# Tree attention on one core: K and Q of heads 16 to 79 laid side by side by GpSimd before TensorE transposes them

## The chip, the cores and the metric

The kernel runs on one core of a Trainium2 chip. A core has five engines that run side by side, each through its own list of instructions in order: TensorE (PE: matmuls and transpositions; its weight loads are shown as PEld), VectorE (DVE), ScalarE (ACT), GpSimd (POOL) and SyncE (SP). Sixteen DMA engines move data between the main memory and the on-chip memory. TensorE writes into PSUM, from where VectorE and ScalarE take its results; everything else lies in SBUF, a memory of 128 partitions.

The metric is the device time of one execution in microseconds (us). The span is the time from the first to the last instruction in the profile; the time of an execution is a little longer.

## The reference

For 8 x 12 = 96 heads, each with 512 positions of 64 numbers, the reference computes softmax attention. A position sees only itself and its ancestors in a binary tree.

```python
for i in range(seq):
    mask[i, i] = 1
    parent = i
    while parent > 0:
        parent = (parent - 1) // 2
        mask[i, parent] = 1

scores = np.einsum('bhqd,bhkd->bhqk', Q, K) * scale
scores = scores + (1 - mask) * (-1e9)

weights = np.exp(scores - np.max(scores, axis=-1, keepdims=True))
weights = weights / (np.sum(weights, axis=-1, keepdims=True) + 1e-10)

return np.einsum('bhqk,bhkd->bhqd', weights, V).astype(np.float32)
```

Inputs and output are float32: 12.6 MB each for Q, K, V and the output.

## The kernel before

**Pairs and steps.** The 96 heads are worked on in 48 pairs, one pair per step `i`. A step has parts that are named by letters: `S` is both score products of pair `i` (`scores1`, `scores2`) with the exponentials on ScalarE, `V` is the value products of pair `i - 1` (`values`, L662) with the normalisation on VectorE (`norm`, L692 and L694), `K` and `Q` are turns. Steps 0 to 8 have lists of their own (`FIRST`); later an odd step is `S V K`, an even one `S V Q`, and step 15 is `S Q V K`. Step 6 is `S K D V Q`: scores of pair 6, a K turn, copies by VectorE, values of pair 5, a Q turn.

**Turns.** The scores need K and Q with the 64 numbers of a position along the partitions. They are loaded with the positions along the partitions, so TensorE transposes them (`turn`, which calls `narrow_k`, `narrow_q`, `wide_k`, `wide_q`, `far_q`), and VectorE copies the result out of PSUM. From pair 8 on a turn serves two pairs. Each transposition loads a piece of K or Q as weights and runs it against a unit matrix. A piece of one head of the pair is 64 columns wide and fills 64 of 128 output partitions; a turn of two pairs takes 16 of these *half* transpositions (L477 for K, L507 and L538 for Q). The K turn in an odd step `i` prepares pairs `i + 3` and `i + 4`, the Q turn in an even step pairs `i + 4` and `i + 5`.

**Blocks and layouts.** K and Q are loaded in blocks of 8 heads: block `b` holds heads `8b` to `8b + 7`, which are pairs `4b` to `4b + 3`. The two heads of a pair do not lie side by side in a loaded block. For blocks 10 and 11 alone `lay_beside` (L445, on GpSimd) copies a block so that they do; the copy takes a buffer of the same pool as the loads. Then one *whole* transposition of 128 columns serves both heads, and a turn takes 8 of them (L470, L532). Heads 0 to 15 are laid out one way, heads 16 to 31 ("wide") a second way, heads 32 to 95 ("far") a third.

**V.** V is loaded in blocks of 16 heads. Before the value products use it, its rows are spread into two working tiles in turn (`vt`, copied at L371 by VectorE, ScalarE and GpSimd). A working tile is written anew for a block only when the values of the block before last are done.

**What sets the order.** The order on each engine is the order in which the program is written; no planner moves anything. GpSimd's own list is written out in `pool_program`: the loads of K, Q and V (which convert float32 to bfloat16 on the way), its share of the spreading, the copies of `lay_beside`, and the stores of finished outputs, in groups of 8 heads. `ready` says from which step on an entry may be emitted; this places it against the other engines' instructions, and GpSimd runs its list strictly in order. `BEHIND` holds the stores back so that loads come first. `NOUT // 2` is the number of output buffers, each of 8 heads. GpSimd's DMAs take eight semaphores in turn, so a DMA waits until the one eight before it has landed. Some of the last stores go out through SyncE's and ScalarE's queues (`store_apart` and the end of the kernel).

The entries of GpSimd's list around the change, before:

```python
(load_q, 28, 4), (load_rows, 2, "leaves0", "leaves1"), (load_k, 32, 8), (load_q, 32, 8),
(load_rows, 3, "upper"),
(spread_pool, (1, "Z0", 8, 16), (1, "Z1", 8, 16), (1, 6, 8, 16), (1, 9, 8, 16)),
(load_q, 40, 8), (load_k, 40, 8), (load_rows, 3, "leaves0", "leaves1"), (load_q, 48, 8),
```

Of the kernel before, what the change touches and what calls it, by code (L numbers as in the profile page):

```python
# [12 lines left out]
NOUT = 22  # L13
# [106 lines left out]
def kernel(  # L120
# [7 lines left out]
    nc = tc.nc  # L128
# [35 lines left out]
    loads = ctx.enter_context(tc.tile_pool(name="loads", bufs=4))  # L164
    vloads = ctx.enter_context(tc.tile_pool(name="vloads", bufs=3))
# [274 lines left out]
    def lay_beside(name, b):  # L440

        kept = ksts if name == "kst" else qsts
        assert all((name, h) in issued for h in range(KB * b, KB * b + KB))
        sides[name, b] = side = loads.tile([P, KB, 4, D], bf16, name=name)
        return nc.gpsimd.tensor_copy(  # L445
            out=side.rearrange("p (s a) t d -> p s a (t d)", a=2).rearrange(
                "p s a (t d) -> p (s a t) d", t=4
            ).rearrange("p (s a) d -> p s a d", a=2).bitcast(int32),
            in_=kept[b].rearrange("p (a x) t d -> p (x t) a d", a=2).bitcast(int32),
        )  # L450

    def both(name, i, slot):

        side = sides[name, i // 4].rearrange("p h t d -> p (h t d)")
        return side[:, 2 * D * slot:2 * D * slot + 2 * D]

    def slots(st, i):
        return st[2 * i // KB].rearrange("p (g x) t d -> p g (x t) d", x=2)

    def wide_k(i):  # L460
        kp = ktp.rearrange("p u c -> p (u c)")
        st = slots(ksts, i)
        place = [2 * i % KB // 2 + a if i < FAR else i % 4 // 2 + 2 * a for a in range(2)]
        for u in range(2):
            for t in range(4):
                mixed = 64 * MIXED[t] + 32 * u
                leaves = 512 + 64 * LEAVES[t] + 32 * u
                dims = (256, 2), (leaves - mixed, 2), (1, 32)
                if ("kst", i // 4) in sides:
                    nc.tensor.transpose(  # L470
                        out=columns(kp, mixed, *dims),
                        in_=both("kst", i, 8 * (i % 4 // 2) + 4 * u + t),
                        identity=ptile[:, 0:128],
                    )
                    continue
                for a in range(2):
                    nc.tensor.transpose(  # L477
                        out=columns(kp[64 * a:64 * a + 64, :], mixed, *dims),
                        in_=st[:, place[a], 4 * u + t, :],
                        identity=ptile[:, 0:128],  # L480
                    )
# [17 lines left out]
    def wide_q(i):  # L499
        qp = qtp.rearrange("p u c -> p (u c)")  # L500
        halves = qp.rearrange("p (b c) -> p b c", b=2)
        st = slots(qsts, i)
        for u in range(2):
            for x, t in enumerate(ORDER):
                c = 256 * u + 64 * x
                for a in range(2):
                    nc.tensor.transpose(  # L507
                        out=halves[64 * a:64 * a + 64, :, c:c + 64],
                        in_=st[:, 2 * i % KB // 2 + a, 4 * u + t, :],
                        identity=ptile[:, 0:128],  # L510
                    )
# [9 lines left out]
    def far_q(i):  # L521
# [5 lines left out]
        st = qsts[j].rearrange("p (g x) t d -> p g (x t) d", x=4)  # L527
        for u in range(2):
            for x, t in enumerate(ORDER):
                c = 128 * u + 32 * x  # L530
                if ("qst", j) in sides:
                    nc.tensor.transpose(  # L532
                        out=quarters[:, :, c:c + 32], in_=both("qst", i, 4 * (2 * last + u) + t),
                        identity=ptile[:, 0:128],
                    )
                    continue
                for a in range(2):
                    nc.tensor.transpose(  # L538
                        out=quarters[64 * a:64 * a + 64, :, c:c + 32],
                        in_=st[:, a, 4 * (2 * last + u) + t, :],  # L540
                        identity=ptile[:, 0:128],
                    )
# [8 lines left out]
    def turn(name, i):  # L551
# [4 lines left out]
        level = (i >= WIDE) + (i >= FAR)  # L556
        {"kst": (narrow_k, wide_k, wide_k), "qst": (narrow_q, wide_q, far_q)}[name][level](i)
# [162 lines left out]
    def pool_program():  # L720
# [17 lines left out]
        for h in range(56, NH, KB):  # L738
# [3 lines left out]
            ops += [(load_q, h, KB)] + top + [(load_k, h, KB)]  # L742
# [25 lines left out]
    def ready(op, i):  # L768
# [158 lines left out]
```

## Time and profile before

| | |
|---|---|
| time, median of 3 runs | 134.0 us (133.42 to 134.24) |
| the profiled execution: its time, its span | 133.38 us, 131.6 us |
| mean granted TensorE clock in it | 0.969 |
| busy: TensorE, VectorE, ScalarE, GpSimd | 114.4, 103.8, 101.1, 83.0 us |
| read from and written to main memory | 37.94 MB, 12.58 MB: 384 GB/s over the span |

The profile page tells how long each engine was busy, the span in 40 slices (each digit is the busy share of a slice in tenths), the chain of work that ended last, and the costliest groups of instructions. A row of the timeline has the start in us, the duration in us, the engine, the line and the operation; behind it, in brackets, how long the engine had been idle just before and what ended that. A row of the windows has, for a stretch of time, the busy time of each engine, the granted clock, the share of the DMA engines and the GB/s that they moved; asked for one engine it has only that one. A row of a group has busy time and mean ns of one instruction, and the idle time just before them.

### The profile page before, as it was taken

To read this page: it belongs to the slowest core of one execution; us is meant where nothing else is said; L and a number is where in the kernel's file an instruction comes from. 1 tells how busy PE (TensorE), PEld (TensorE's weight loads), DVE (VectorE), ACT (ScalarE), POOL (GpSimd) and SP (SyncE) were. 2 spreads that over 40 slices of the span, in tenths; PEclk is the share of its full clock that TensorE was granted. 3 is DMA by queue.
4 is the path that set the end of the run, shared out by engine and by line. 5 is a ranking of instruction groups with operands and counts; after the bars stand their busy time and mean duration, and the time that the engine had idled before them with its cause. 6 is when DMAs were issued, how large, how long until landed. Compare 5 with 4: busy or idle time off the path is not lost.

```text
span 131.6 us, 5435 instructions
## 1 busy us (share of the span) xinstructions
PE 114.4 (87%) x2353; PEld 79.7 (61%) x2353; DVE 103.8 (79%) x254; ACT 101.1 (77%) x163; POOL 83.0 (63%) x114
## 2 busy tenths in 40 slices
PE   6788959999999798899998898997998999999900
PEld 2354745676667566577676575675675777775600
DVE  3459859588999998989899879898899977875440
ACT  4279577689799996959996878896898888789900
POOL 6999524454485999994498799944999935002000
PEclk9999996799999999999999999999999999999975
DMA  2999999999999999999999999999999999999991
GB/s 87 244 195 194 200 196 200 201 202 206 203 201 209 207 207 204 210 206 202 209 206 200 306 269 207 293 282 242 330 221 327 246 288 400 403 398 396 395 345 66
DMA packets 28157, 32.25 MB, mean 245 GB/s; under 512 B 1214, under 2 KB 23358, under 8 KB 28134
## 3 DMA queue, kind: packets, MB, share of 16 engines
q0 software_dynamic: 25696, 29.63, 110.7%
q1 hardware_dynamic: 1878, 1.83, 4.0%
q10 hardware_dynamic: 560, 0.46, 1.3%
q8 instruction: 18, 0.29, 0.8%
q14 instruction: 5, 0.04, 0.1%
HBM read 37.94 MB, written 12.58 MB: 384 GB/s over the span
## 4 chain that ended last, share of the span: by engine, by line
DMA 30%; PE 29%; POOL 17%; DVE 13%; issue 4%; ACT 2%; POOLq 0%; ACTq 0%
DMA kst<-in_K_dram 22%; PE ob L662 9%; POOL vt L371 9%; DMA vst<-in_V_dram 8%; PE s L567 4%; DVE of L694 4%; DVE vt L371 3%; PE s L574 3%; POOL kst L244 2%; POOL qst L244 2%; PE s L612 2%; PE s L601 2%; POOL vst L244 2%; PE qtp L532 2%; PE ktp L470 2%
## 5 line engine op out<-in xcount | busy, mean ns | idle before, releaser
L584 ACT ACTIVATE e<-s 128x1024 bf16<-128x1024 f32 x40 | 40.9, 1022 | 13.2 <-PE s L574 12.7
L662 PE MATMUL ob<-vt,e 128*128 128x65 bf16 (+1 forms) x940 | 37.4, 198 | 1.6 <-DVE of L694 1.1
L662 PEld LDWEIGHTS <-e 128*128 128x128 bf16 (+1 forms) x960 | 30.4, 103 | 9.5 <-PE s L612 1.1
L371 POOL COPY vt<-vst 32x512 int32<-32x512 int32 (+4 forms) x44 | 32.5, 740 | 5.2 <-PE ob L662 3.0
L618 ACT ACTIVATE e<-s 128x384 bf16<-128x384 f32 x80 | 34.7, 490 | 0.0
L694 DVE TENSOR_TENSOR of<-ob,rec 128x512 f32<-128x512 f32 x47 | 32.5, 692 | 1.6
L371 DVE COPY vt<-vst 32x1024 bf16<-32x1024 bf16 (+5 forms) x47 | 21.4, 456 | 2.6 <-DMA vst<-in_V_dram 1.8
L692 DVE RECIPROCAL rec<-ob 128x8 f32<-128x8 f32 x47 | 9.6, 205 | 10.7 <-PE ob L662 9.8
L702 POOL DMA_DIRECT2D out_dram<-of x11 | 9.9, 898 | 9.1 <-DVE of L694 8.7
L574 PE MATMUL s<-qq,kq 64*128 64x512 bf16 x80 | 15.3, 377 | 0.0
L612 PE MATMUL s<-qq,kq 64*128 64x160 bf16 (+1 forms) x320 | 14.8, 208 | 0.4 <-issue 0.4
L612 PEld LDWEIGHTS <-kq 64*128 64x128 bf16 x320 | 12.3, 94 | 4.7 <-issue 0.6
L567 PE MATMUL s<-far,codes 40*128 40x512 bf16 x64 | 12.5, 386 | 0.1
L580 ACT ACTIVATE e<-s 128x1024 bf16<-128x1024 f32 x8 | 8.2, 1022 | 5.6 <-PE s L574 5.5
L254 POOL DMA_DIRECT2D qst<-in_Q_dram x12 | 8.4, 704 | 6.3 <-DMA kst<-in_K_dram 3.4
L601 PEld LDWEIGHTS <-codes 40*128 40x128 bf16 x80 | 6.4, 94 | 9.5 <-issue 3.9
L543 DVE COPY qq<-qtp 128x1024 bf16<-128x1024 bf16 x16 | 10.9, 682 | 0.7 <-PE qtp L538 0.7
L254 POOL DMA_DIRECT2D kst<-in_K_dram x11 | 8.4, 764 | 4.3 <-DMA vst<-in_V_dram 1.7
L477 PE MATMUL ktp<-ptile,kst 128*64 128x128 bf16 x256 | 9.9, 220 | 1.2 <-DMA kst<-in_K_dram 0.6
L601 PE MATMUL s<-far,codes 40*128 40x384 bf16 x64 | 10.6, 324 | 0.4 <-ACT e L618 0.3
L371 ACT COPY vt<-vst 32x512 int32<-32x512 int32 (+3 forms) x19 | 10.4, 546 | 0.6 <-DMA vst<-in_V_dram 0.2
L299 POOL DMA_DIRECT2D vst<-in_V_dram x7 | 5.6, 800 | 6.4 <-DMA vst<-in_V_dram 4.5
(56 smaller groups left out, 157.2 us busy)
## 6 DMA issues: line engine op xcount, KB each, us to landing
out_dram<-of POOLq DMA_DIRECT2D x10, 1024.0 KB, 16.4
kst<-in_K_dram POOLq DMA_DIRECT2D x9, 512.0 KB, 14.3
qst<-in_Q_dram POOLq DMA_DIRECT2D x8, 512.0 KB, 16.3
vst<-in_V_dram POOLq DMA_DIRECT2D x12, 256.0 KB, 14.0
vst<-in_V_dram POOLq DMA_DIRECT2D x6, 512.0 KB, 13.0
qst<-in_Q_dram POOLq DMA_DIRECT2D x6, 256.0 KB, 12.1
kst<-in_K_dram POOLq DMA_DIRECT2D x4, 256.0 KB, 10.8
out_dram<-of SPq DMA_DIRECT2D x3, 256.0 KB, 6.0
```

What stands on the lines that cost most here:

```text
L254: return nc.gpsimd.dma_start(out=kept[b][:, h0 % KB:h0 % KB + n, :, :].rearrange("p (g x) t d -> p g (x t d)", x=x), in_=src[:, h0 // x:(h ...
L371: return copy(out=dst, in_=src)
L477: nc.tensor.transpose(out=columns(kp[64 * a:64 * a + 64, :], mixed, *dims), in_=st[:, place[a], 4 * u + t, :], identity=ptile[:, 0:128],)
L543: nc.vector.tensor_copy(out=qqs[j][:, :, 8 * last:8 * last + 8, :].rearrange("p b u c -> p b (u c)"), in_=quarters,)
L567: nc.tensor.matmul(out=sp[:, a, :], lhsT=(k1code if i < WIDE else k1wide)[64 * a:64 * a + CODE_ROWS, :], rhs=(q1code, q1wide, q1far)[(i >= ...
L574: nc.tensor.matmul(out=sp[:, a, :], lhsT=keys(i, a, TOP), rhs=qTs[i][64 * a:64 * a + 64, :, :].rearrange("p t c -> p (t c)"), start=False, ...
L584: ) if i < WIDE else nc.scalar.activation(
L601: nc.tensor.matmul(out=flat[:, a, :, :].rearrange("p u (t c) -> p u t c", t=4)[:, :, :, 32 // n:], lhsT=k2wide[64 * a:64 * a + CODE_ROWS, ...
L612: nc.tensor.matmul(out=flat[:, a, :, lo:hi], lhsT=keys(i, a, WTILE2[t]), rhs=qT[64 * a:64 * a + 64, :, lo:hi], start=False, stop=t == 1, s ...
L618: nc.scalar.activation(out=e2s[i % NE][:, a, :, 32:128].rearrange("p t (r u) -> p t r u", u=n), in_=flat[:, a, :, :].rearrange("p u (t r) ...
L662: nc.tensor.matmul(out=ob[lo:hi, a, 65 * t:65 * t + 65], lhsT=e[:, a, PLACE[t], lo:hi], rhs=vt[vtile[tile_v][0]][:, head(i, a) % VB, vtile ...
L694: nc.vector.tensor_tensor(out=ofs[j][:, h0:h1 + 1:head(i, 1) - head(i, 0), :, :], in0=o4[:, a:a + n, :, 0:D], in1=rec[:, a:a + n, :, :].to ...
```

## The change

GpSimd lays K and Q of blocks 2 to 9 side by side too, as it did with blocks 10 and 11. The copies get a pool of their own (`beside`, two buffers for K and two for Q). The blocks of heads 16 to 31 are laid in two halves, because there the two heads of a pair lie closer together. With this `wide_k`, `wide_q` and `far_q` lose their path of half transpositions: every turn from pair 8 on takes 8 whole ones. TensorE has 4204 instructions for 4720. GpSimd's list gets the new entries: blocks 2 to 5 at written places, then for each block `b` from 8 on the laying of Q and K of block `b - 2`, just behind the load of Q of block `b` and ahead of the spreading of V and the load of K. The load of Q of heads 56 to 63 moves ahead of rows of V of heads 64 to 79. The output buffers go from 11 to 9.

```diff
-NOUT = 22
+NOUT = 18
...
+    beside = ctx.enter_context(tc.tile_pool(name="beside", bufs=2))
...
-        sides[name, b] = side = loads.tile([P, KB, 4, D], bf16, name=name)
-        return nc.gpsimd.tensor_copy(
-            out=side.rearrange("p (s a) t d -> p s a (t d)", a=2).rearrange(
-                "p s a (t d) -> p (s a t) d", t=4
-            ).rearrange("p (s a) d -> p s a d", a=2).bitcast(int32),
-            in_=kept[b].rearrange("p (a x) t d -> p (x t) a d", a=2).bitcast(int32),
-        )
+        sides[name, b] = side = beside.tile([P, 16, 2, D], bf16, name=f"{name}side")
+        if KB * b >= 2 * FAR:
+            return nc.gpsimd.tensor_copy(
+                out=side.bitcast(int32),
+                in_=kept[b].rearrange("p (a x) t d -> p (x t) a d", a=2).bitcast(int32),
+            )
+        for m in range(2):
+            nc.gpsimd.tensor_copy(
+                out=side[:, 8 * m:8 * m + 8, :, :].bitcast(int32),
+                in_=kept[b][:, 4 * m:4 * m + 4, :, :].rearrange(
+                    "p (a x) t d -> p (x t) a d", a=2
+                ).bitcast(int32),
+            )
...
     def wide_k(i):
...
-                for a in range(2):
-                    nc.tensor.transpose(
-                        out=columns(kp[64 * a:64 * a + 64, :], mixed, *dims),
-                        in_=st[:, place[a], 4 * u + t, :],
-                        identity=ptile[:, 0:128],
-                    )
+                nc.tensor.transpose(
+                    out=columns(kp, mixed, (256, 2), (leaves - mixed, 2), (1, 32)),
+                    in_=both("kst", i, 8 * (i % 4 // 2) + 4 * u + t),
+                    identity=ptile[:, 0:128],
+                )
...
     def wide_q(i):
...
-                for a in range(2):
-                    nc.tensor.transpose(
-                        out=halves[64 * a:64 * a + 64, :, c:c + 64],
-                        in_=st[:, 2 * i % KB // 2 + a, 4 * u + t, :],
-                        identity=ptile[:, 0:128],
-                    )
+                nc.tensor.transpose(
+                    out=halves[:, :, c:c + 64], in_=both("qst", i, 8 * (i % 4 // 2) + 4 * u + t),
+                    identity=ptile[:, 0:128],
+                )
...
-            (load_rows, 3, "upper"),
+            (lay_beside, "kst", 2), (lay_beside, "qst", 2), (load_rows, 3, "upper"),
             (spread_pool, (1, "Z0", 8, 16), (1, "Z1", 8, 16), (1, 6, 8, 16), (1, 9, 8, 16)),
-            (load_q, 40, 8), (load_k, 40, 8), (load_rows, 3, "leaves0", "leaves1"), (load_q, 48, 8),
+            (load_q, 40, 8), (load_k, 40, 8), (lay_beside, "kst", 3), (lay_beside, "qst", 3),
+            (load_rows, 3, "leaves0", "leaves1"), (load_q, 48, 8),
             (spread_top, 2), (spread_pool, (2, "Z0", 0, 16), (2, "Z1", 0, 16)), (load_k, 48, 8),
-            (spread_pool, (2, "X", 0, 16), (2, "M", 0, 16), (2, "D1", 0, 16)), (spread_top, 3, 0, 12),
+            (lay_beside, "kst", 4), (lay_beside, "qst", 4),
+            (spread_pool, (2, "X", 0, 16), (2, "M", 0, 16), (2, "D1", 0, 16)),
+            (load_q, 56, 8), (lay_beside, "qst", 5), (lay_beside, "kst", 5), (spread_top, 3, 0, 12),
             (load_rows, 4, "upper"), (spread_top, 3, 12, 16),
...
-            ops += [(load_q, h, KB)] + top + [(load_k, h, KB)]
+            beside = [(lay_beside, name, h // KB - 2) for name in ("qst", "kst")]
+            ops += ([(load_q, h, KB)] + beside if h > 56 else []) + top + [(load_k, h, KB)]
...
         if f is lay_beside:
-            return 2 * (i + 3) >= KB * (args[1] + 2) + KB - 4 * KB
+            return args[1] < 4 or i >= 4 * args[1] - 8
...
         if f is load_rows:
-            return 2 * i >= VB * (args[0] - 2)
+            return i >= {4: 12, 5: 17}.get(args[0], 8 * (args[0] - 2))
```

More of the change, by code (lines that the diff above doesn't have):

```diff
@@ L443, in lay_beside @@
         assert all((name, h) in issued for h in range(KB * b, KB * b + KB))
-        sides[name, b] = side = loads.tile([P, KB, 4, D], bf16, name=name)
-        return nc.gpsimd.tensor_copy(
-            out=side.rearrange("p (s a) t d -> p s a (t d)", a=2).rearrange(
-                "p s a (t d) -> p (s a t) d", t=4
-            ).rearrange("p (s a) d -> p s a d", a=2).bitcast(int32),
-            in_=kept[b].rearrange("p (a x) t d -> p (x t) a d", a=2).bitcast(int32),
-        )
+        sides[name, b] = side = beside.tile([P, 16, 2, D], bf16, name=f"{name}side")
[11 more added lines that the diff above has]
+            )
     def both(name, i, slot):
[L454 to L458, printed above, removed]
+        return sides[name, i // 4][:, slot, :, :].rearrange("p a d -> p (a d)")
     def wide_k(i):
         kp = ktp.rearrange("p u c -> p (u c)")
-        st = slots(ksts, i)
-        place = [2 * i % KB // 2 + a if i < FAR else i % 4 // 2 + 2 * a for a in range(2)]
         for u in range(2):
@@ L467, in wide_k @@
                 leaves = 512 + 64 * LEAVES[t] + 32 * u
[L468 to L472, printed above, removed]
-                        identity=ptile[:, 0:128],
-                    )
-                    continue
-                for a in range(2):
-                    nc.tensor.transpose(
-                        out=columns(kp[64 * a:64 * a + 64, :], mixed, *dims),
-                        in_=st[:, place[a], 4 * u + t, :],
-                        identity=ptile[:, 0:128],
-                    )
+                nc.tensor.transpose(
[3 more added lines that the diff above has]
+                )
         kk = work.tile([P, 2, 20, 32], bf16, name="kq")
@@ L501, in wide_q @@
         halves = qp.rearrange("p (b c) -> p b c", b=2)
-        st = slots(qsts, i)
         for u in range(2):
@@ L530, in far_q @@
                 c = 128 * u + 32 * x
[L531 to L542, printed above, removed]
+                nc.tensor.transpose(
+                    out=quarters[:, :, c:c + 32], in_=both("qst", i, 4 * (2 * last + u) + t),
+                    identity=ptile[:, 0:128],
+                )
         nc.vector.tensor_copy(
@@ L556, in turn @@
         level = (i >= WIDE) + (i >= FAR)
+        assert not level or (name, i // 4) in sides, (name, i)
         {"kst": (narrow_k, wide_k, wide_k), "qst": (narrow_q, wide_q, far_q)}[name][level](i)
```

4 lines of the change are left out of this document (removed).

## The prediction

> **What bounds the kernel now.** I read the page first (its parts 1 and 2), then the chain of waits, then the timeline of TensorE and GpSimd around the places that the chain names.
>
> ```profile
> PE 114.4 (87%) x2353; PEld 79.7 (61%) x2353; DVE 103.8 (79%) x254; ACT 101.1 (77%) x163; POOL 83.0 (63%) x114
> POOL 6999524454485999994498799944999935002000
> DMA  2999999999999999999999999999999999999991
> ```
>
> The DMA row is full from the second slice to the last but one: the transfers never run dry. TensorE has the most busy time, and GpSimd (POOL), the engine that the change loads, is the least busy. But its row is uneven: slices 14 to 18, 21 to 26 and 29 to 32 are nearly full.
>
> ```profile
> 65.02 18.93 DMA kst<-in_K_dram
> 84.00 0.64 PE ktp L477 x16
> ...
> 90.39 0.61 POOL vt L371
> ...
> 99.85 1.05 POOL qst L445
> 100.94 0.62 PE qtp L532 x8
> ```
>
> In the chain a K load is issued at 65.02 and lands 18.9 us later; TensorE then turns it at 84.00. From 90.39 to 100.9 the chain runs on GpSimd: it spreads V for heads 80 to 95, then lays Q block 10 beside itself (L445), and TensorE starts on that block right behind it.
>
> ```profile
> 81.42 0.68 PE L538 MATMUL qtp<-ptile,qst 128*64 128x128 bf16 x16 [0.61 <-DMA qst<-in_Q_dram]
> 93.84 0.64 PE L477 MATMUL ktp<-ptile,kst 128*64 128x128 bf16 x16 [0.29 <-DMA kst<-in_K_dram]
> 100.94 0.62 PE L532 MATMUL qtp<-ptile,qst 128*128 128x128 bf16 x8 [0.60 <-POOL qst L445]
> 120.00:125.00 5.00, 4.88 (x102) 3.30 (x98) 2.47 (x6) 4.58 (x9) 0.59 (x1) 1.00 1.01 392
> 128.00:132.00 4.00, 0.00 (x0) 0.00 (x0) 0.00 (x0) 0.00 (x0) 0.00 (x0) 0.50 0.22 75
> ```
>
> So three things are nearly level here. TensorE meets Q block 8 at 81.42 and K block 9 at 93.84 just as they land; it meets Q block 10 at 100.94 just as GpSimd has laid it; and from there it is busy without a hole (4.88 of 5.00 us in the window from 120) while the DMA share stays at 1.01. No gain in one of them alone can shorten the span by much; a delay of GpSimd's laying reaches TensorE at once.
>
> **The change part by part.**
>
> *Transpositions.* 32 turns (16 of K, 16 of Q, for blocks 2 to 9) go from 16 half transpositions to 8 whole ones: 256 pairs of weight load and matmul fewer. Blocks 10 and 11 are laid already, so both kinds stand in this trace:
>
> ```profile
> 85.47 0.79 PE L662 MATMUL ob<-vt,e 128*128 128x65 bf16 x20
> 86.10 0.61 PE L538 MATMUL qtp<-ptile,qst 128*64 128x128 bf16 x16
> 86.64 0.39 PE L567 MATMUL s<-far,codes 40*128 40x512 bf16 x2
> ...
> 102.40 0.79 PE L662 MATMUL ob<-vt,e 128*128 128x65 bf16 x20
> 103.12 0.62 PE L470 MATMUL ktp<-ptile,kst 128*128 128x128 bf16 x8
> 103.67 0.39 PE L567 MATMUL s<-far,codes 40*128 40x512 bf16 x2
> ...
> 105.29 0.62 PE L532 MATMUL qtp<-ptile,qst 128*128 128x128 bf16 x8
> ```
>
> From start to start, 16 halves take 86.64 - 86.10 = 0.54 us, 8 wholes 103.67 - 103.12 = 0.55. And the value products ahead of them hold TensorE 0.63 us with halves behind, 0.72 with wholes. A turn thus gets no cheaper, but 0.1 us dearer: 32 turns, at most 3 us, all of it inside the waits below, so I put nothing in the sum for it.
>
> The Trainium skill's page "TensorE: Matmul & The Clock Gate", section "Back-to-back issue gap", gives about 81 ns per load-and-matmul pair at 128 columns in a stream; by it 8 pairs fewer would save an estimated 0.65 us a turn. The trace has 34 ns for a half and 69 for a whole, so here the count of instructions is not what a turn costs. The Trainium skill's page "TensorEngine Tiling (Array Packing)", section "Key Properties", says that two column tiles load and multiply in parallel and that a change of tiling drains the array, and the value products end on 64-column tiles; both speak against this change, and the 0.54 beside 0.55 and the 0.63 beside 0.72 agree.
>
> *Copies.* GpSimd gets 20 more: 8 of half a block (blocks 2 and 3), 12 of a whole one (blocks 4 to 9).
>
> ```profile
> L445 POOL COPY kst<-kst 128x1024 int32<-128x1024 int32 x2 | 2.1, 1046 | 1.7 <-DMA kst<-in_K_dram 1.7
> L371 POOL COPY vt<-vst 32x512 int32<-32x512 int32 x18 | 11.2, 621 | 3.9 <-PE ob L662 3.0
> 32.63:84.74 52.11, 41.65 (x59) 1.00 1.25 219
> ```
>
> A whole one is 1.05 us by its own row. A half one has no row; bounds are half of that, 0.52, and 0.62, the row of another copy of the same length; I take 0.62. Together 12 x 1.05 + 8 x 0.62 = 17.5 us on GpSimd, in order with its loads and its spreading.
>
> *The first wait.* The copies of block 2 stand behind the issue of the Q load of heads 32 to 39. In the built program each GpSimd DMA waits for the one eight before it to land.
>
> ```profile
> 26.98 0.64 PE L477 MATMUL ktp<-ptile,kst 128*64 128x128 bf16 x16
> ...
> 19.84 0.70 POOL L254 DMA_DIRECT2D qst<-in_Q_dram  x1 [0.65 <-DMA kst<-in_K_dram]
> DMA to landing us min/median/max: 11.5/11.5/11.5
> ...
> 31.93 0.70 POOL L254 DMA_DIRECT2D qst<-in_Q_dram  x1 [0.51 <-PE s L612]
> ```
>
> For that load the one eight before was issued at 19.84 and took 11.5 us: it landed at 31.3, the load went out from 31.93 to 32.63, and earlier it cannot go. The first half of K block 2 is then laid at 33.3. TensorE turned that K at 26.98 (pairs 8 and 9, step 6) straight from the load. Now it waits for 33.3: 6.3 us. Behind this turn in TensorE's order stand the values of pair 5, the Q turn and all scores; VectorE's copies, ScalarE's exponentials and the stores wait for those.
>
> *The second wait, which covers the first.* From 32.63 on GpSimd has no pause left. Its work of before up to the issue of Q block 10's load (84.04 to 84.74) is 41.65 us in that window; the after kernel puts 8 halves (5.0) and 9 wholes (Q and K of 4 to 7, Q of 8; 9.4) among it before Q block 8 is laid. With the pause of 0.04 to 0.06 us that the timeline has between two copies (some 45 times, 2 us): 32.6 + 41.65 + 5.0 + 9.4 + 2 = 90.7, so TensorE turns Q block 8 at about 91.0 where it did at 81.42: 9.6 us later. TensorE itself, 6.3 us late, would have been there at about 87 (80.8 without its own wait, plus 6.3), so it waits some 4 us more. The idle time of 10.5 us in that window (52.11 - 41.65) was all the room that GpSimd had, and the added 16.4 us don't fit in.
>
> *The third wait.* Four steps later the chain of before is met again.
>
> ```profile
> 90.39 4.86 POOL L371 COPY vt<-vst 32x512 int32<-32x512 int32 x6 [3.04 <-PE ob L662]
> ```
>
> GpSimd may spread V for heads 80 to 95 only when the values of pair 31 are done; then follow 6 copies, the load of K block 11, 3 copies, a store and the laying of Q block 10, and TensorE goes on at 100.94: 10.55 us. After: Q block 8 at 91.0, four steps of 2.18 us (from 103.12 to the next such turn at 105.29 it is 2.17) give 99.7; the values are done 0.2 earlier, 99.5; plus 10.6 is 110.1. TensorE alone would be there at 108.4, so it waits 1.7 us; before, the same place cost 0.60. Later blocks have room: Q block 11 is needed four steps on.
>
> *The tail.* From this turn to the end of the span it was 131.6 - 100.94 = 30.7 us, TensorE without a hole. It is the same work after, so the span is 110.1 + 30.7 = 140.8. The profiled execution has 1.8 us around its span (133.38 for 131.6): **142.6 us**, +9.2 on the profiled execution, which lies 0.6 us under the median of 134.0. I say 142.5.
>
> *At nothing.*
>
> ```profile
> 59.84 0.91 POOL L702 DMA_DIRECT2D out_dram<-of  x1
> out_dram<-of POOLq DMA_DIRECT2D x10, 1024.0 KB, 16.4
> 79.48 0.77 POOL L254 DMA_DIRECT2D kst<-in_K_dram  x1
> DMA to landing us min/median/max: 14.3/14.3/14.3
> ...
> 95.21 0.77 POOL L254 DMA_DIRECT2D kst<-in_K_dram  x1
> DMA to landing us min/median/max: 13.9/13.9/13.9
> ...
> 111.82 0.62 PE L470 MATMUL ktp<-ptile,kst 128*128 128x128 bf16 x8
> ```
>
> Two output buffers fewer: the tenth block of outputs (pairs 36 to 39, from about 101) now waits for the first store, issued at 59.84 with some 16.4 us to land: 25 us of room; only a store that much later would cost, and the same sum as above puts it 8 later. K and Q buffers free earlier: loads are held by the eight-before rule, not by buffers. Q block 7's load is moved ahead of V rows of heads 64 to 79: the same bytes through a full queue. K block 9's load goes out at 85.6 by the sum, 6.1 late, of 14.3 us to land, most of which is queue: it is hidden. K block 11's goes out at 105.4, 10.2 late of 13.9; here the queue runs dry for some us, and K block 11 lands perhaps 3 us late, at 112; it is needed at 111.8 + 9.2 = 121. If this cover were gone, the 3 us would show.
>
> **The rivals.**
>
> 1. *Only the last chain stays* (GpSimd's copies go quicker than I add, or fit into its pauses). K block 9 still lands no earlier than 93.8, by the wait of TensorE for it at 93.84; its laying, 1.05 us, stands ahead of the spreading of heads 80 to 95: 94.9 + 10.6 = 105.5 for 100.94, +4.5: **137.9**. For it: TensorE and VectorE could win back what step 6 lost. Against: the sum of rows has no such room.
>
> 2. *GpSimd hinders VectorE.*
>
> ```profile
> L371 DVE COPY vt<-vst x12: 416/532/909, 62.4 to 97.7; 32x1024 bf16<-32x1024 bf16 x12
> L371 DVE COPY vt<-vst 32x1024 bf16<-32x1024 bf16 x28 | 14.7, 527 | 1.0 <-DMA vst<-in_V_dram 0.4
> ```
>
> The same copy took 416 to 909 ns while GpSimd was busy about it. If all 28 such copies took 0.909 for their mean of 0.527, VectorE had 10.7 us more; between none and all of it would show, I take half, 5: **147.5**. The Trainium skill's page "Advanced Engine Details and Errata", section "VectorE Performance Modes", says that the second port is shared and that both block each other. The spread of that row agrees; what it costs is not seen.
>
> 3. *Faster: the instruction count rules.* If a whole transposition cost the 34 ns of a half one, a turn would fall by 0.27 us, 32 turns by 8.7 us.
>
> ```profile
> 125.00:128.00 3.00, 0.34 (x10) 0.17 (x5) 1.35 (x5) 0.00 (x0) 0.00 (x0) 0.81 0.97 355
> ```
>
> TensorE would then regain the lost steps, and the end would be the queue's: it is still full here (0.97), and 0.22 x 4.00 = 0.9 us of transfers are left behind 128. Packed they end at 128.9, so between 0 and 2.7 us are to be had; I take half, 1.4: **132.0**. It decides from the point at which GpSimd lays a block before TensorE asks for it, which at 26.98 against 33.3 it doesn't, and the two transposition rows speak against the price.
>
> 4. *The change does nothing measurable*, because waits and gains cancel under the full queue: **134**. The build has 4204 TensorE instructions for 4720, so it is made; only the 6.3 us at step 6 would have to vanish.
>
> **How the numbers follow.** Forecast 0.68 (140 to 146), rival 1 0.14, rival 2 0.11, rival 3 0.03, rival 4 0.04. The range goes from 137.5 (rival 1, with 0.4 for its copies) to 147.5 (rival 2), which leaves out 3 and 4 and the edges. About 1% is what a measurement of this kernel can tell from no change. Slower by over 1%: 0.93; within: 0.04; faster: 0.03.
>
> **What will show it.** Right, if TensorE's first whole K turn waits some 6 us for GpSimd, if Q block 8 is turned near 91 behind GpSimd, if GpSimd's row is full from slice 10 to 32 with about 100 us busy, and if 8 wholes again take 0.55. The DMA row should have its first holes after slice 30. Wrong, if GpSimd's copies of 128 partitions take far from 1.05, if it shows pauses between 33 and 90, or if TensorE regains its steps between 35 and 80.

## The result, and the profile after

The changed kernel takes 146.07 us (median of 6 runs, 144.66 to 146.61) where the kernel before takes 133.78 us (6 runs on the same chip): a ratio of 1.0905, 95% interval 1.0869 to 1.0942. It is slower by 12.3 us. Forecast were 142.5 us, from 137.5 to 147.5. The profiled execution took 146.32 us with a span of 144.5. In some kernels below the executions scatter by 1 to 3%; the ratios leave out those that lie over 1.5% above the fastest of their kernel, while medians and ranges take in all, so that the two need not agree.

First the page of the changed kernel: busy times, three rows of the span in 40 slices (3.6 us each), and the chain that ended last.

```profile
PE 119.1 (82%) x2097; PEld 83.8 (58%) x2097; DVE 109.0 (75%) x254; ACT 101.1 (70%) x163; POOL 100.2 (69%) x134
POOL 7989353556999999929999999995199995200200
PEclk9999999965999999699999999969999999999997
DMA  4999999999999999998999999999993999993473
POOL 30%; PE 24%; DMA 22%; DVE 16%; issue 4%; ACT 2%; POOLq 0%; ACTq 0%
```

GpSimd is busy 17.2 us more (100.2 for 83.0), and its row is full from slice 11 to 33, but for two breaks (18, and 28 and 29). It is the first engine of the chain, with 30%. The DMA row, full to the end before, now has a hole in slice 31 (108.4 to 112.0 us) and thins out from slice 37 on: the loads run out while GpSimd is late to issue the next (K block 11, in the timeline at 108.92). TensorE has 256 pairs of instructions fewer and is still busy 4.7 us longer (119.1 for 114.4). The PEclk row tells most of the reason: it drops to 5 or 6 in three places ahead of the end (slices 9 and 10, 17, 27); before, it drops to 6 and 7 in one (slices 7 and 8). The whole transpositions have a part in it too: in the experiment below that has them without any copy TensorE is busy 115.4 us at a granted clock of 0.983, in the kernel before with fewer output buffers 112.7 at 0.984.

Next the waits of the changed kernel (us in all, times, the longest).

```profile
PE ktp L469 <- POOL kstside L452: 7.5, 1, 7.5
POOL vt L372 <- PE ob L643: 7.3, 2, 4.8
PE qtp L519 <- POOL qstside L447: 4.0, 2, 2.6
```

TensorE waits three times for a laid block, 7.5 us once and 4.0 in two. GpSimd in turn waits twice for TensorE, 7.3 us. In the timeline (start, duration, engine, line; in brackets the idle time before and what ended it) these are the places:

```profile
31.85 0.70 POOL L255 DMA_DIRECT2D qst<-in_Q_dram  x1 [0.43 <-issue]
32.55 1.17 POOL L452 COPY kstside<-kst 128x512 int32<-128x512 int32 x2
33.23 1.03 PE L469 MATMUL ktp<-ptile,kstside 128*128 128x128 bf16 x8 [7.55 <-POOL kstside L452]
36.22 0.85 POOL L300 DMA_DIRECT2D vst<-in_V_dram  x1 [1.40 <-issue]
64.25 1.38 POOL L372 COPY vt<-vst 32x128 int32<-32x128 int32 x4 [2.58 <-PE ob L643]
93.02 1.03 POOL L447 COPY qstside<-qst 128x1024 int32<-128x1024 int32 x1
94.11 0.62 PE L519 MATMUL qtp<-ptile,qstside 128*128 128x128 bf16 x8 [2.57 <-POOL qstside L447]
104.15 4.81 POOL L372 COPY vt<-vst 32x512 int32<-32x512 int32 x6 [4.76 <-PE ob L643]
108.92 0.77 POOL L255 DMA_DIRECT2D kst<-in_K_dram  x1
113.59 1.07 POOL L447 COPY qstside<-qst 128x1024 int32<-128x1024 int32 x1
114.72 0.62 PE L519 MATMUL qtp<-ptile,qstside 128*128 128x128 bf16 x8 [1.48 <-POOL qstside L447]
```

TensorE stands from 25.68 until the first half of K block 2 is laid, then before Q block 8 and before Q block 10. Between the first two, GpSimd stops only at 36.22 and at 64.25. The second stop is for the values of pair 15, which TensorE delivers 11.3 us later than before (step 16 in the table below).

The granted clock, by windows (the last columns are PEclk, DMA share and GB/s):

```profile
29.81:36.64 6.83, 3.41 (x40) 2.79 (x42) 2.29 (x7) 0.00 (x0) 4.16 (x7) 0.50 1.32 203
57.12:60.53 3.41, 3.41 (x44) 2.37 (x42) 3.16 (x7) 2.41 (x4) 3.14 (x6) 0.50 1.18 205
94.66:98.07 3.41, 3.41 (x43) 2.35 (x41) 2.60 (x4) 2.25 (x4) 3.41 (x5) 0.50 1.07 338
```

Behind waits TensorE runs at half speed: 10.2 us of its busy time lie in these windows (3.41 in each), where the granted clock is 0.50. By the clock alone, the same work at the full one would take about half of that, an estimate. From the score matmul of step 29 (94.66) to that of step 30 (98.28) it takes 3.62 us, to the next (100.46) the usual 2.18:

```profile
94.66 0.61 PE L548 MATMUL s<-far,codes 40*128 40x512 bf16 x2
98.28 0.39 PE L548 MATMUL s<-far,codes 40*128 40x512 bf16 x2
100.46 0.39 PE L548 MATMUL s<-far,codes 40*128 40x512 bf16 x2
```

The start of the first score matmul of some steps, before and after, shows where the time was lost (the column on the right is an experiment below):

| step | before | after | lost | after, TensorE kept busy in two waits |
|---|---|---|---|---|
| 7 | 28.71 | 36.18 | 7.5 | 35.54 |
| 16 | 51.54 | 62.81 | 11.3 | 62.18 |
| 28 | 79.08 | 89.84 | 10.8 | 89.19 |
| 29 | 82.03 | 94.66 | 12.6 | 94.00 |
| 30 | 84.57 | 98.28 | 13.7 | 96.18 |
| 37 | 101.49 | 115.27 | 13.8 | 113.92 |
| 47 | 122.28 | 136.77 | 14.5 | 134.98 |
| span | 131.6 | 144.5 | 12.9 | 141.9 |

### The profile page after: what moved, and what is told of

Its sections match the earlier page's. It is cut to its first block, busy times and chain, and to the rows that moved or that the text cites. A ratio compares the mean times of both kernels' runs of the same rounds, so it can differ in the third digit from the quotient of the medians.

```text
span 144.5 us, 4942 instructions
## 1 busy us (share of the span) xinstructions
PE 119.1 (82%) x2097; PEld 83.8 (58%) x2097; DVE 109.0 (75%) x254; ACT 101.1 (70%) x163; POOL 100.2 (69%) x134
## 4 chain that ended last, share of the span: by engine, by line
POOL 30%; PE 24%; DMA 22%; DVE 16%; issue 4%; ACT 2%; POOLq 0%; ACTq 0%
DMA vst<-in_V_dram 17%; POOL vt L372 14%; PE ob L643 8%; DVE vt L372 6%; DMA kst<-in_K_dram 5%; DVE of L675 4%; PE qtp L519 3%; PE s L548 3%; POOL qstside L447 3%; PE ktp L469 2%; PE s L555 2%; PE s L593 2%; POOL kst L255 2%; POOL qst L255 2%; PE s L582 2%
## 5 line engine op out<-in xcount | busy, mean ns | idle before, releaser
L643 PE MATMUL ob<-vt,e 128*128 128x65 bf16 (+1 forms) x940 | 38.5, 200 | 4.1 <-DVE of L675 2.5
L643 PEld LDWEIGHTS <-e 128*128 128x128 bf16 (+1 forms) x960 | 31.5, 104 | 12.2 <-DVE of L675 3.3
L372 DVE COPY vt<-vst 32x1024 bf16<-32x1024 bf16 (+5 forms) x47 | 26.9, 571 | 3.0 <-DMA vst<-in_V_dram 2.1
L469 PE MATMUL ktp<-ptile,kstside 128*128 128x128 bf16 x160 | 13.1, 228 | 7.9 <-POOL kstside L452 7.5
L683 POOL DMA_DIRECT2D out_dram<-of x11 | 9.8, 891 | 12.3 <-DVE of L675 12.3
L673 DVE RECIPROCAL rec<-ob 128x8 f32<-128x8 f32 x47 | 9.6, 204 | 11.3 <-PE ob L643 10.9
L593 PEld LDWEIGHTS <-kq 64*128 64x128 bf16 x320 | 12.3, 96 | 4.8 <-issue 0.6
L469 PEld LDWEIGHTS <-kstside 128*128 128x128 bf16 x160 | 9.7, 102 | 8.8 <-POOL kstside L452 7.7
L478 DVE COPY kq<-ktp 128x256 bf16<-128x256 bf16 x20 | 8.3, 415 | 8.3 <-PE ktp L469 8.3
L519 PE MATMUL qtp<-ptile,qstside 128*128 128x128 bf16 x128 | 10.3, 226 | 4.0 <-POOL qstside L447 4.0
L372 ACT COPY vt<-vst 32x512 int32<-32x512 int32 (+3 forms) x19 | 10.4, 545 | 1.2 <-DMA vst<-in_V_dram 0.8
## 6 DMA issues: line engine op xcount, KB each, us to landing
vst<-in_V_dram POOLq DMA_DIRECT2D x12, 256.0 KB, 10.8
vst<-in_V_dram POOLq DMA_DIRECT2D x6, 512.0 KB, 11.3
kst<-in_K_dram POOLq DMA_DIRECT2D x4, 256.0 KB, 10.2
```

Of the source, the lines that this page charges most:

```text
L372: return copy(out=dst, in_=src)
L469: nc.tensor.transpose(out=columns(kp, mixed, (256, 2), (leaves - mixed, 2), (1, 32)), in_=both("kst", i, 8 * (i % 4 // 2) + 4 * u + t), id ...
L519: nc.tensor.transpose(out=quarters[:, :, c:c + 32], in_=both("qst", i, 4 * (2 * last + u) + t), identity=ptile[:, 0:128],)
L593: nc.tensor.matmul(out=flat[:, a, :, lo:hi], lhsT=keys(i, a, WTILE2[t]), rhs=qT[64 * a:64 * a + 64, :, lo:hi], start=False, stop=t == 1, s ...
L643: nc.tensor.matmul(out=ob[lo:hi, a, 65 * t:65 * t + 65], lhsT=e[:, a, PLACE[t], lo:hi], rhs=vt[vtile[tile_v][0]][:, head(i, a) % VB, vtile ...
```

## The experiments

The theory: the time is lost in waits for blocks that GpSimd lays late, in a list that it runs in order; the clock goes down behind waits. The rivals: GpSimd's copying hinders VectorE by itself; the new transpositions cost or gain; the output buffers. Ratios are to the kernel before, timed beside it.

**The transpositions alone.** `lay_beside` is left out, and the whole transpositions read the loads as they lie.

```diff
-        return sides[name, i // 4][:, slot, :, :].rearrange("p a d -> p (a d)")
+        kept = ksts if name == "kst" else qsts
+        flat = kept[i // 4].rearrange("p h t d -> p (h t d)")
+        return flat[:, 2 * D * slot:2 * D * slot + 2 * D]
```

> The changed kernel without any laying: the 8 whole transpositions of a turn read the loaded block as it lies, so K and Q go to the scores in a wrong order; no copy is made, none is waited for. It measures the form of the transpositions alone. Theory: 8 wholes cost TensorE as much as 16 halves and 0.1 us more a turn: 133.5 to 136, no gain. Rival (the count of instructions is what a turn costs): 132.5 or less, and a step of 1.9 us instead of 2.1.

132.84 us, ratio 0.9946 (0.9904 to 0.9988), just under the 133.5 to 136 that I had expected. The timeline of this kernel, in a stretch without waits:

```profile
112.34 0.39 PE L549 MATMUL s<-far,codes 40*128 40x512 bf16 x2
114.51 0.39 PE L549 MATMUL s<-far,codes 40*128 40x512 bf16 x2
```

A step takes 2.18 us with whole transpositions; with halves the shortest take 2.07. Fewer instructions don't make a step shorter. The half per cent that this kernel gains lies close to what can be told from no change, and it has neither the four copies of before nor the new ones.

**No laying at all, halves everywhere** (the kernel before without the copies of blocks 10 and 11).

```diff
-        return ops
+        return [op for op in ops if op[0] is not lay_beside]
```

> The kernel before without any laying: blocks 10 and 11 too are transposed in halves straight from their loads. Theory (a whole transposition saves nothing and costs 0.1 us a turn, the laying of Q block 10 holds TensorE for 0.6 us): steps 37 to 43 take 2.09 us and not 2.18, TensorE ends some 1.2 us earlier, the full transfer queue gives back part of it: 132.3 to 133.4 for 133.6. Rival (whole transpositions were a gain in the last blocks): 134.5 or more.

133.37 us, ratio 1.0016 (0.9997 to 1.0035). The page:

```profile
PE 112.5 (85%) x2414; PEld 78.9 (60%) x2417; DVE 103.6 (79%) x254; ACT 101.2 (77%) x163; POOL 79.6 (60%) x110
DMA  2999999999999999999999999999999999999992
```

GpSimd is busy 3.4 us less than before, and nothing comes of it. TensorE's 112.5 us for 114.4 are no gain from it: the next kernel, which lays blocks 10 and 11 as before, has 112.7 us, and both profiles lack the half clock of slices 7 and 8 that the one before has. Nor does TensorE end earlier, as I had expected: step 47 starts at 123.60, before at 122.28. The DMA row is full, and the span is that of before, 131.6 us. So there seems to have been little to gain here for a change that eases TensorE.

**Two output buffers fewer alone** (before, `NOUT = 18` for 22).

> The kernel before with 9 output buffers for 11, alone. Theory: the tenth buffer's store has landed 25 us before it is needed; no change, 133 to 134.5. Rival (VectorE waits for stores): 135 or more.

133.29 us, ratio 0.9999 (0.997 to 1.0029): nothing.

**The copies alone.** GpSimd's list of the changed kernel, with all copies; TensorE turns halves straight from the loads, so nothing waits for a copy.

```diff
-                nc.tensor.transpose(
...
+                if False:
+                    nc.tensor.transpose(
...
+                for a in range(2):
+                    nc.tensor.transpose(
```

(The same in all three places that turn K or Q; the first branch is never taken.)

> GpSimd's program is that of the changed kernel, all 24 copies included, but nobody reads what they write: TensorE transposes in halves straight from the loads. It takes the wait for the laid block away and leaves GpSimd's load. Theory (the loss is in the waits for laid blocks): TensorE meets Q block 8 at 84 to 87 and Q block 10 at about 101 to 103; 134.5 to 137.5. Rival (a full GpSimd alone costs, by late loads and late spreading, or by slower copies on VectorE): 140 or more.

137.09 us (135.27 to 139.27), ratio 1.0169 (1.0146 to 1.0192). The profiled execution is the one of 139.27 us. Groups of VectorE by form, first this kernel, then the changed one (busy us, mean ns):

```profile
L373 DVE COPY vt<-vst 32x1024 bf16<-32x1024 bf16 x28 | 18.4, 658 | 0.9 <-DMA vst<-in_V_dram 0.4
```

```profile
L372 DVE COPY vt<-vst 32x1024 bf16<-32x1024 bf16 x28 | 18.1, 646 | 1.9 <-DMA vst<-in_V_dram 1.4
```

Before, these 28 took 527 ns each. So with 20 copies more on GpSimd the copies of VectorE are about a quarter slower, whether or not anybody waits for what GpSimd copies. By the ratio GpSimd's load by itself is worth 1.7%, by the median of all four runs 2.8%; most of the 9.1% needs somebody who waits for the laid blocks.

How the load can cost time is seen in the profiled execution. Three copies of VectorE that took 1.02 us before (first row) take 2.20 while GpSimd lays Q block 2 and spreads V; the value products wait for them:

```profile
33.75 1.02 DVE L371 COPY vt<-vst 32x1024 bf16<-32x1024 bf16 x3
34.42 2.20 DVE L373 COPY vt<-vst 32x1024 bf16<-32x1024 bf16 x3
36.68 0.89 PE L676 MATMUL ob<-vt,e 128*128 128x65 bf16 x20 [1.68 <-DVE vt L373]
```

A stretch of 6.8 us at a granted clock of 0.50 follows, then another wait for VectorE of 1.64 us and a second stretch. Step 16 begins at 57.60 for 51.54, 6.1 us later, with no wait for a laid block. The executions of 135.27 and 135.85 us can't have lost that much in the end, and no profile shows them.

**One wait at a time.** Three kernels lay only some of the blocks, in the places that the changed kernel has for them; the other blocks are turned by halves. First only blocks 2, 3, 10 and 11:

```diff
+LAID = (2, 3, 10, 11)
...
+                if ("kst", i // 4) in sides:
...
-        return ops
+        return [op for op in ops if op[0] is not lay_beside or op[2] in LAID]
```

> The changed kernel with only blocks 2, 3, 10 and 11 laid. The first wait stays (7.5 us, and a slower clock behind it), GpSimd has 12 copies fewer. Theory that the second wait covers the first but that the first alone would also cost: TensorE loses some 8 us at step 6 and wins back at most the 2.5 us that it waited for transfers before: 138 to 140. Rival (the lost time is won back by step 36, and only the full GpSimd counts): 134 to 135.5.

142.14 us, ratio 1.0653 (1.0619 to 1.0687).

```profile
33.53 1.03 PE L475 MATMUL ktp<-ptile,kstside 128*128 128x128 bf16 x8 [7.55 <-POOL kstside L453]
30.08:36.91 6.83, 3.38 (x40) 0.50 1.32 202
```

The first wait and its half clock are there in full, and blocks 2 and 3 alone are worth 6.5%: eight copies of 0.6 us, for the first of which TensorE stands 7.55 us. That is more than the 138 to 140 that I had expected: TensorE is 7.8 us late at step 7, wins nothing back, and is 10.4 us late at step 16.

Then blocks 4 to 11, without the first wait (`LAID = range(4, 12)`), in two experiments:

> The changed kernel, with blocks 2 and 3 transposed in halves straight from their loads again: GpSimd has 8 half copies fewer and TensorE has nothing to wait for at step 6. Theory (GpSimd full, then the chain behind the landing of K block 9): the first wait is gone; Q block 8 is laid 4.9 us earlier than in the sum, at about 86, and Q block 10 at about 105; some 138.5 us (137.5 to 140.5). Rival (the first wait and the slow clock behind it are the whole loss): 134 to 136. Rival (whole transpositions and copies hinder TensorE and VectorE everywhere): 142 or more.

> Blocks 4 to 11 are laid, once more. By the waits: TensorE stands about 5.5 us before K block 4 at about 45 and some 3.4 us before Q block 8 at about 87, each with a stretch of half clock of 6.8 us; 141 to 142.5 us. By a rival, in which the half clock came by itself in that one execution: the waits, and no half clock behind them, 137 to 139.

142.25 us, ratio 1.0628 (1.0569 to 1.0687), not the 138.5 that I had expected; the single execution of the second experiment took 141.63. The time is what I had given to a rival, that whole transpositions and copies hinder everywhere (142 or more), but the transpositions alone cost nothing and the copies alone 1.7%. The timeline and windows of the second (TensorE alone: busy, PEclk, DMA share, GB/s):

```profile
50.97 1.03 PE L475 MATMUL ktp<-ptile,kstside 128*128 128x128 bf16 x8 [5.25 <-POOL kstside L448]
90.58 0.62 PE L545 MATMUL qtp<-ptile,qstside 128*128 128x128 bf16 x8 [3.47 <-POOL qstside L448]
47.62:54.45 6.83, 3.48 (x38) 0.50 1.23 207
92.00:95.41 3.41, 3.41 (x41) 0.50 1.09 326
```

My expectation took away one wait and kept the others as they were. But TensorE, now on time, comes to K block 4 before it is laid and stands there for 5.25 us: a wait that the changed kernel doesn't have, because there the first one has made TensorE late enough. Waits cover each other, so they don't add: 6.5% for blocks 2 and 3, 6.3% for blocks 4 to 11, and 9.1% for both.

Then only blocks 8 to 11 (`LAID = range(8, 12)`), in two experiments:

> The changed kernel with only blocks 8 to 11 laid (before: 10 and 11), blocks 2 to 7 in halves. Theory: GpSimd has time, and only the laying of K block 9 behind its landing, ahead of the spreading of V for heads 80 to 95, is left: Q block 10 some 4.5 us later than before, 138 us (136.5 to 139). Rival (the first wait, or a full GpSimd, is the whole loss): 133.5 to 134.5.

> Only blocks 8 to 11 are laid, once more. By the waits: TensorE stands about 5.4 us before Q block 8 from about 81, since GpSimd lays that block only behind the spreading of V, at 85.3; 138 to 139 us, and the same places as before. By a rival, in which that wait came from a late landing in one execution: no wait there, and a time of 135 to 136.

138.53 us, ratio 1.0373 (1.0334 to 1.0412); 138.98 in the second experiment, whose timeline is:

```profile
81.11 2.77 POOL L373 COPY vt<-vst 32x1024 int32<-32x1024 int32 x3
83.83 0.91 POOL L716 DMA_DIRECT2D out_dram<-of  x1
84.73 0.70 POOL L256 DMA_DIRECT2D qst<-in_Q_dram  x1
85.48 1.03 POOL L448 COPY qstside<-qst 128x1024 int32<-128x1024 int32 x1
86.57 1.03 PE L545 MATMUL qtp<-ptile,qstside 128*128 128x128 bf16 x8 [6.90 <-POOL qstside L448]
97.19 4.80 POOL L373 COPY vt<-vst 32x512 int32<-32x512 int32 x6 [1.91 <-PE ob L676]
```

The time was as expected, but not by the cause that I had in mind (the last chain, behind K block 9). GpSimd is not overloaded here: Q block 8 waits because three spreading copies, a store and a load stand ahead of it in the list. TensorE stands 6.90 us (5.42 in the profile of the first experiment), and the spreading of heads 80 to 95 starts at 97.19 for 90.39.

**The place in the list.** If so, moving the one copy must help. In the kernel with blocks 8 to 11, Q block 8 is laid two spreading copies, a store and a load earlier:

```diff
-                ops.append((spread_pool, *[(o, part, 0, 16) for part in ("X", "M", "D1")]))
+                ops.append((spread_pool, (o, "X", 0, 16)))
+                if h == 72:
+                    ops.append((lay_beside, "qst", 8))
+                ops.append((spread_pool, *[(o, part, 0, 16) for part in ("M", "D1")]))
```

(The copy of Q block 8 at its old place is left out.)

> Blocks 8 to 11 alone are laid, and Q block 8 is laid two spreading copies, a store and a load earlier in GpSimd's list, as soon as it has landed (81.6). By the place in GpSimd's list: TensorE turns Q block 8 at about 83 for 86.4, with at most one stretch of half clock behind it; then the laying of K block 9 at its landing (94.8), which stands ahead of the spreading of heads 80 to 95, sets the next wait: spreading from 95.9, Q block 10 at 105.5 to 106.5, 136 to 137.3 us. By the amount of copying (the same copies, in whatever place, hinder the others): 138 to 138.8, no change against blocks 8 to 11 as they were.

And the same with K block 9 turned by halves, without its copy:

> As with Q block 8 laid earlier, and K block 9 is not laid but turned from its load by halves: 7 copies are left. By the place in GpSimd's list: the spreading of heads 80 to 95 no longer stands behind K block 9; it starts with the values of pair 31, at about 92.5, Q block 10 at 102.5 to 103.5, 134 to 135.3 us. By the amount of copying: one copy of 1.05 us in eight fewer, at most 0.6 us less than blocks 8 to 11, 138.

The first took 139.46 us (137.21 to 140.57, before 134.0), ratio 1.0282 (1.022 to 1.0345). The median of its four times lies above both expectations and is no lower than that of blocks 8 to 11, and the interval touches theirs, so by its time this kernel doesn't settle it. Its profile, of the execution of 140.45 us, has the places as expected: the wait before Q block 8 is down to 2.04 us,

```profile
82.59 1.04 PE L545 MATMUL qtp<-ptile,qstside 128*128 128x128 bf16 x8 [2.04 <-POOL qstside L448]
```

the spreading starts at 96.01 behind K block 9, and Q block 10 is laid from 105.43. But now TensorE waits 3.54 us for that block, and 6.8 us at half clock follow. The second kernel took 136.66 (134.17 to 138.48), ratio 1.0194 (1.0136 to 1.0251), clearly under 1.0373; its median lies between the two expectations. Its profiled execution is the one of 134.17 us:

```profile
80.89 1.11 POOL L448 COPY qstside<-qst 128x1024 int32<-128x1024 int32 x1
82.06 1.03 PE L545 MATMUL qtp<-ptile,qstside 128*128 128x128 bf16 x8 [2.04 <-POOL qstside L448]
92.99 4.80 POOL L373 COPY vt<-vst 32x512 int32<-32x512 int32 x6 [1.12 <-PE ob L676]
102.42 1.07 POOL L448 COPY qstside<-qst 128x1024 int32<-128x1024 int32 x1
```

There the steps are where the place predicts them: the wait before Q block 8 is 2.04 us for 6.90 (or 5.42), the spreading starts at 92.99 (expected 92.5), Q block 10 is laid from 102.42. One copy moved and one left out are together worth 1.8%; the runs don't divide this between the two. Why the other executions of these two kernels are 2 to 4 us longer stays open.

**The half clock alone.** The changed kernel, with matmuls whose results nobody uses put into the first and the second wait (28 ahead of the K turn in step 6, 9 ahead of the Q turn in step 28).

```diff
+            if step == "Q" and i == 28:
+                spin("s1", 9)
...
+            if step == "Y":
+                spin("s1", 28)
```

> The changed kernel, with matmuls of zeros on TensorE in two of its waits: 28 of 512 columns ahead of the K turn of step 6 and 9 ahead of the Q turn of step 28. Their results are not used. It keeps TensorE busy while it waits and so tells what the half clock behind the waits costs. Theory (3 to 4 us of the loss is the half clock; of the first wait's part most is hidden by the full GpSimd): no half clock at 30 to 36 and at 95, step 29 takes 2.2 us and not 3.6; 143 to 145 in place of 146. Rival (the waits alone are the loss): 145.5 to 146.5.

143.94 us, ratio 1.081 (1.0789 to 1.0831), for 1.0905 (1.0869 to 1.0942).

```profile
33.83 0.62 PE L469 MATMUL ktp<-ptile,kstside 128*128 128x128 bf16 x8 [0.48 <-POOL kstside L452]
94.00 0.39 PE L548 MATMUL s<-far,codes 40*128 40x512 bf16 x2
96.18 0.39 PE L548 MATMUL s<-far,codes 40*128 40x512 bf16 x2
55.99:59.40 3.41, 3.41 (x42) 0.50 1.16 208
```

The waits are about as long as they were (the first K turn at 33.83 for 33.23), but the clock stays up behind them: step 29 takes 2.18 us for 3.62. One stretch at half clock is left, at 55.99. By the medians 2.1 us, by the ratios 1.3 us, are thus not waiting but slow running after two of the waits, less than the 3 to 4 that I had put on it.

## Why the prediction was right, and where it was off

The direction was right and the time within the range, 3.6 us above the forecast of 142.5. It lies just above the 140 to 146 of the forecast itself; what the range holds beyond that came from rival 2.

*Transpositions*: right. 8 wholes take 94.66 - 94.11 = 0.55 us from their start to that of the scores behind them, and the whole turns alone make no step shorter. Rival 3, that the count of instructions rules, is out.

*Copies*: right. 20 copies added 17.2 us to GpSimd (17.5 forecast).

*The first wait*: right in place, cause and size: K block 2 is laid and turned at 33.23 (33.3), 6.25 us later than before, behind the load of Q that is issued at 31.85. The half clock behind it, which the sum didn't have, brings the loss to 7.5 us at step 7.

*The second wait, which covers the first*: right in kind, 3.1 us short: Q block 8 is turned at 94.11, not at 91.0. GpSimd's work was as added up, but not "has no pause left":

```profile
32.55:93.02 60.47, 54.64 (x75) 0.94 1.19 214
```

The columns are the busy time of GpSimd, PEclk, DMA share and GB/s. With the laying of Q block 8 (1.03) it is 55.67 us of work, where the sum had 56.05 (41.65 + 5.0 + 9.4); the pauses are 60.47 - 54.64 = 5.83 us, where I took 2. Two of them, 1.40 and 2.58, make 3.98; a pause between 33 and 90 was among the prediction's own signs of being wrong. The larger is GpSimd waiting for the values of pair 15, 11.3 us later than before. The first wait with its half clock accounts for 7.5 of these. By an estimate from these numbers, with 7.5 alone the values would have been done 3.8 us earlier, and GpSimd, which was ready 2.58 us earlier, would not have paused: the pause needs both parts. The other 3.8 us are lost between steps 7 and 16, where the prediction put nothing:

```profile
41.40 2.05 DVE L372 COPY vt<-vst 32x1024 bf16<-32x1024 bf16 x3
52.28 2.01 DVE L372 COPY vt<-vst 32x1024 bf16<-32x1024 bf16 x2
```

Before, these copies of VectorE took 1.02 and 1.04 us (33.75, 42.93). Now GpSimd lays Q block 3 beside the first, and lays Q block 4 and then spreads V beside the second. TensorE waits for VectorE, 0.90 us at 43.51 and 1.71 at 55.30; the stretch at half clock at 57.12 follows. No run takes these 3.8 us apart, but the profiled execution of the kernel with the copies alone, its longest, loses 6.1 us up to step 16 in the same way. I treated the two waits as one covering the other; in fact the first wait, together with the slower copies of VectorE, feeds the second through the spreading of V. The same losses make TensorE itself late: it is ready for Q block 8 at 94.11 - 2.57 = 91.54, where the prediction had it at about 87. Had GpSimd been as early as forecast, TensorE would have been the later of the two, so that a forecast for this place came near is in part luck.

*The third wait*: right as a chain, wrong by what goes before. From the spreading at 104.15 to the turn at 114.72 it is 10.6 us, as forecast. But it starts at 104.15, where the sum had 99.5: 3.1 us from the second wait, and 1.4 from step 29 at half clock, which the sum didn't have at all (0.1 is left over). The step of the prediction that failed here is "four steps of 2.18 us": one of them took 3.62.

*The tail*: 144.5 - 114.72 = 29.8 us, 30.7 forecast; from the start of step 47 to the end of the span it is 7.7 us for 9.3, and no run shows what shortened it. 3.1 + 1.4 + 0.1 - 0.9 = 3.7 us is what the span lies above the forecast of 140.8.

*At nothing*: the output buffers are confirmed by the kernel with `NOUT = 18`. The late loads of K were hidden too: among the waits of the changed kernel TensorE has none for K block 9 or 11.

*Rival 1*, only the last chain, fell: the waits ahead of that chain stay, and its condition, that GpSimd's copies fit into its pauses, isn't met. *Rival 2*, GpSimd hinders VectorE, is there beside the forecast rather than in its place: VectorE's 28 copies took 18.1 us for 14.7, and the kernel with the copies alone loses 1.7%. I had given it 5 us as a case of its own. The Trainium skill's page "Advanced Engine Details and Errata", section "VectorE Performance Modes", says that the two share a port and block each other; the rows agree, with 646 ns for 527. How much of the 12.3 us this is can't be read off: it is part of the 3.8 us above, and the rest lies inside the waits.

## What to carry to other kernels

Before work goes to an engine that is idle on average, write down where in its list the work will stand and when the consumer asks for it: eight copies of 0.6 us, behind a load that went out no earlier than 31.85, cost 6.5% here, while the same engine had 37% of its time free. A copy belongs in the list at the point where its input lands: for Q block 8 that took the wait from 6.90 us to 2.04. Take waits together, not one by one: without the first, the next one appears. Ask whom the copying engine slows down meanwhile, here VectorE. And price a turn from start to start in the trace, not by its count of instructions.

## What the runs showed of the hardware

Short waits take TensorE's clock down. In the middle of the traces shown above a stretch at half clock lasts 3.41 us or twice that (6.83); in the profile of the first experiment with blocks 8 to 11 one lasts about 10.2. In the changed kernel the three followed idle times of 7.55, 1.71 and 2.57 us, while none followed the 1.48 us before 114.72. Matmuls put into the first and the last of the three waits kept the clock up there, so at these two places the idle time is the cause; at the second it is only what came before. The timeline row of the second, and the window behind the 2.04 us in the kernel with Q block 8 laid early and K block 9 not laid:

```profile
55.30 0.79 PE L643 MATMUL ob<-vt,e 128*128 128x65 bf16 x20 [1.71 <-DVE of L675]
```

```profile
81.81:85.22 3.41, 3.15 (x32) 0.50 1.19 279
```

The Trainium skill's page "TensorE: Matmul & The Clock Gate", section "What's actually happening", has a window of 3413 ns that runs by itself: the lengths agree. Its section "HAM oscillation — how this bites in real kernels" gives the rule that no idle gap should be over some 3.4 us; here stretches followed three gaps under it, of 1.71, 2.04 and 2.57 us, and the last was gone when its gap was filled, so the rule is too kind for this kernel.

VectorE's copies from SBUF to SBUF slow down when GpSimd copies beside them, 527 ns to 646 in the mean of the most frequent form; in the three kernels here with no more copying than before the mean is 531 to 546. The mean understates what a chain pays that meets the worst of them: the three copies at 34.42 in the kernel with the copies alone took 2.20 us for 1.02. The longest single copy tells little: it took 909 ns before and 1507 in the changed kernel, but 1122 to 1264 in those three kernels.
